# A hybrid decoder layer on one core: S5 tables made earlier and stored in longer runs, the last stage's weights split once

## The chip, the core and the metric

The kernel runs on one core of one Trainium2 chip. The metric is the time of one execution on the device in microseconds. TensorE (PE) multiplies matrices, VectorE (DVE), ScalarE (ACT) and GpSimd (POOL) work on elements, and SyncE (SP) issues the DMAs. All names in capitals are those of the profile.

## The reference

One layer with 2048 tokens of 1024 channels in float32. The input is normalized and projected to 8716 columns; three branches use them: A, a diagonal complex state space model (S5) with 32 groups of 16 channels and 64 states each; B, dilated window attention; C, a Mamba-2 SSD scan. Each branch is gated, projected, weighed by a sigmoid gate and summed; one more projection is added to the input. Cut to what matters:

```python
h = rms_norm(x, norm_w)
proj = h @ w_in
(u_a, z_a, q, k, v, z_b, xbc, dt, z_c, gate_logits) = split(proj, ...)
y_a = s5_mixer(u_a, ...) * silu(z_a)
y_b = attention_mixer(q, k, v, ...) * silu(z_b)
y_c = ssd_mixer(xbc, dt, z_c, ...)
gates = sigmoid(gate_logits)              # three of 1024 columns
merged = g0 * (y_a @ proj_a) + g1 * (y_b @ proj_b) + g2 * (y_c @ proj_c)
return x + merged @ w_out

def s5_mixer(u, ...):
    lam, f = ...                          # per group and state, complex
    bu = einsum(f * b, u)
    h[t] = lam * h[t - 1] + bu[t]         # a scan over 2048 tokens
    y = real(einsum(c, h)) + d * u
    g = gelu(y)
    return g * sigmoid(g @ glu_w + glu_b)
```

## The kernel before

**Precision.** Every large matmul is made in three passes of fp32r: each operand is split in a high part (rounded, made on ACT) and a low part (the rest, made on DVE), and TensorE adds high x high, low x high and high x low (L373 to L375, L384 to L386, L1267 to L1269).

**The projection** runs in two halves of 1024 tokens, in units of one output tile each; a unit is 24 matmuls, with 256 or 512 columns. For each weight tile one DMA of 1 MB brings the raw columns (`wr_q`, `wr_k`, `wr_g`, ..., L345), ACT casts them to the high part (L360), DVE makes the low part (L361). Outputs go to DRAM (`q_d`, `k_d`, `v_d`, `ua_d`, `g_d`, ...).

**Branch work between the units.** `main` calls `run` with jobs (work, its steps, first unit, last unit), and the steps of a job are spread evenly over these units. In this way the S5 parameters come first (`s5_setup`, units 2 to 38), then attention and the SSD chunks of the first half (`ssd(0)`, units 73 to 135), h of the second half (`a0_early`, from unit 84), then in the second half the S5 branch itself (`s5`, units 153 to 180), its GLU, attention, and SSD chunks (`ssd(1)`). The final order of each engine's instructions is set by the compiler's scheduler from this program; all DMAs stand in one queue on SP, in program order as it was scheduled, and use eight semaphores in turn.

**S5.** `s5_setup` writes a table `tab_d` of [128, 32 groups, 163 columns] to DRAM with ten DMAs, each in a slice of 16 to 19 columns, that is, in runs of 64 to 76 bytes (L935, L940, L952, L967, L1015). `s5` works in eight blocks of four groups. For each it loads the table (`s5t`), and `cplx` (L1042 to L1044) makes three sets of complex products, with two POOL multiplies and one DVE add each; TensorE turns one of them (`s5pp`) and makes the lag kernels from another (`s5kp`, L1062), which go through DRAM (`ks_d`). The phasors `wt` take eight POOL multiplies (L1102, L1103) and four DVE operations (L1104) a block. Then, group by group: a matmul (`s5i`, L1112), the turn back on DVE and POOL, a scan on DVE (L1121), the turn forward, and two matmuls (`s5yp`, L1132 and L1133).

**SSD.** For each chunk, POOL makes the rows `sr` (L806) that TensorE needs for `sd` (L811); their results go on to `syd`, `syo`, `ssp` on TensorE.

**The last stage** (`final`) does four time blocks of 512 tokens. Each has eight projection steps: a step loads 128 columns of `proj_a`, `proj_b`, `proj_c` as three DMAs (`fr`, 768 KB), splits them on ACT (L1197, L1257) and DVE (L1198, L1258), does 36 matmuls of 512 columns (`fp`, L1267 to L1269), and weighs the three results by the gates `fg`, loaded from `g_d` (L1264), on DVE (L1270) and POOL (L1272). Then come four output steps: 1 MB of `w_out` (`or`), four splits, 96 matmuls of 256 columns (`op`, L1302 to L1304). The same weights are loaded and split anew in each of the four time blocks. SSD chunks and the attention merge of the second half run beside its first blocks (`last`).

## Time and profile before

| | |
|---|---|
| time, median of 3 runs | 2605.06 us (2604.53 to 2605.40) |
| span of the profiled execution | 2611.2 us, 40810 instructions |
| busy: PE, DVE, ACT, POOL | 2477.1, 1465.2, 888.8, 718.3 us |
| DMA | 354.90 MB in 463591 packets, mean 136 GB/s |

The profile is of one execution of its own; its span is its time, and there is no other figure for it. PE's busy time is the whole time in which it had a matmul under way. PEclk is the TensorE clock that was granted, as a part of full speed. DMA share is the mean busy share of the 16 DMA engines. "Idle before" names what ended the idle time of the engine ahead of an instruction.

### The profile page before, as it was taken

Reading aid. Unit: us, or ns where it says so; the run is one execution under the profiler, and the core shown is the slowest. Engines: PE = TensorE matmul, PEld = TensorE weight load, DVE = VectorE, ACT = ScalarE, POOL = GpSimd, SP = SyncE. Lnnn points to the kernel's source line nnn. Section 1 sums busy time; section 2 is a strip of 40 time slices with the busy share of each in tenths; the row PEclk is TensorE's granted clock in tenths of the full one; section 3 lists DMA queues with packets and bytes.
Section 4 is the critical chain, followed back from the end, with each engine's and each line's share of the span. In section 5 each row is a group of like instructions: output and inputs, shape, how many; then the busy total and the mean of one; then the engine's idle time right before and its main releaser. Section 6 shows DMA issues by size and latency. Waiting matters only on the chain. (4 is left out here: it accounts for less than half of the span.)

```text
span 2611.2 us, 40810 instructions
## 1 busy us (share of the span) xinstructions
PE 2477.1 (95%) x15216; PEld 2173.1 (83%) x15216; DVE 1465.2 (56%) x3153; ACT 888.8 (34%) x1956; POOL 718.3 (28%) x737
## 2 busy tenths in 40 slices
PE   8778999999999999978889999999999999999999
PEld 8778998888888888877789998888888779797888
DVE  6652255643433335488986546642333887878663
ACT  4122234543233224212225335443332433333331
POOL 2121000002333324288862100000010343534221
PEclk8988999999999999999999999999999999999999
DMA  7995332433445335343336432443343667675664
GB/s 156 90 56 117 100 108 83 138 117 108 134 145 158 119 103 166 81 111 106 101 97 198 127 119 90 138 138 105 117 137 123 212 201 218 200 214 169 204 201 133
DMA packets 463591, 354.90 MB, mean 136 GB/s; under 512 B 132641, under 2 KB 420641, under 8 KB 463393
## 3 DMA queue, kind: packets, MB, share of 16 engines
q1 hardware_dynamic: 463392, 352.29, 50.6%
q8 instruction: 121, 1.98, 0.3%
q14 instruction: 78, 0.63, 0.1%
HBM read 239.79 MB, written 112.41 MB: 135 GB/s over the span
## 5 line engine op out<-in xcount | busy, mean ns | idle before, releaser
L384 PE MATMUL ps_g<-hT_hi,wh_g 128*128 128x512 f32 x768 | 310.0, 404 | 0.0
L386 PE MATMUL ps_g<-hT_hi,wl_g 128*128 128x512 f32 x768 | 305.6, 398 | 0.0
L385 PE MATMUL ps_g<-hT_lo,wh_g 128*128 128x512 f32 x768 | 305.0, 397 | 0.0
L806 POOL TENSOR_TENSOR sr<-tle,ahl 128x384 fp32r<-128x384 f32 x128 | 116.3, 930 | 519.9 <-PE sd L811 388.5
L386 PEld LDWEIGHTS ps_g<-hT_hi,wl_g 128*128 128x128 f32 x768 | 144.5, 188 | 33.1
L385 PEld LDWEIGHTS ps_g<-hT_lo,wh_g 128*128 128x128 f32 x768 | 144.5, 188 | 32.3
L384 PEld LDWEIGHTS ps_g<-hT_hi,wh_g 128*128 128x128 f32 x768 | 144.4, 188 | 32.2
L1272 POOL TENSOR_TENSOR fm<-fm,fg 128x512 f32<-128x512 f32 x64 | 96.0, 1500 | 209.7 <-DVE fg L1270 172.6
L361 DVE TENSOR_TENSOR wl_g<-wr_g,wh_g 128x512 fp32r<-128x512 f32 x96 | 71.0, 759 | 116.1 <-ACT wh_g L360 106.3
L659 ACT ACTIVATE sm<-sm,ml 128x256 f32<-128x256 f32 (+1 forms) x192 | 86.4, 451 | 136.1 <-DVE ml L657 111.9
L373 PE MATMUL ps_q<-wh_q,hT_hi 128*128 128x256 f32 x384 | 112.5, 294 | 18.0 <-ACT e_q L424 17.6
L384 PE MATMUL ps_xbc<-hT_hi,wh_xbc 128*128 128x512 f32 x320 | 129.0, 403 | 0.0
L385 PE MATMUL ps_xbc<-hT_lo,wh_xbc 128*128 128x512 f32 x320 | 128.6, 402 | 0.0
L386 PE MATMUL ps_xbc<-hT_hi,wl_xbc 128*128 128x512 f32 x320 | 128.4, 401 | 0.0
L373 PE MATMUL ps_v<-wh_v,hT_hi 128*128 128x256 f32 x384 | 110.7, 291 | 13.2 <-ACT e_v L414 10.8
L374 PE MATMUL ps_v<-wl_v,hT_hi 128*128 128x256 f32 x384 | 112.9, 295 | 9.5 <-DVE wl_v L361 9.5
L563 ACT ACTIVATE e_g<-ps_g 128x512 f32<-128x512 f32 x96 | 56.9, 595 | 182.3 <-PE ps_g L386 173.8
L498 DVE SCALAR_TENSOR_TENSOR ac_cv<-xb_cv,convw,ac_cv 128x512 f32<-128x512 f32 x120 | 90.3, 752 | 48.9 <-ACT ac_cv L496 48.2
L374 PE MATMUL ps_k<-wl_k,hT_hi 128*128 128x256 f32 x384 | 112.0, 292 | 5.8 <-DVE wl_k L361 5.7
L374 PE MATMUL ps_q<-wl_q,hT_hi 128*128 128x256 f32 x384 | 112.5, 294 | 4.6 <-DVE wl_q L361 4.6
L373 PE MATMUL ps_k<-wh_k,hT_hi 128*128 128x256 f32 x384 | 112.1, 294 | 4.8 <-ACT e_k L424 4.8
L375 PE MATMUL ps_q<-wh_q,hT_lo 128*128 128x256 f32 x384 | 113.4, 296 | 3.3 <-DVE hT_lo L317 3.3
(627 smaller groups left out, 7552.5 us busy)
## 6 DMA issues: line engine op xcount, KB each, us to landing
wr_g<-in_w_in_dram SPq DMA_DIRECT2D x24, 1024.0 KB, 5.3
g_d<-e_g SPq DMA_DIRECT2D x96, 256.0 KB, 2.4
fg<-g_d SPq DMA_DIRECT2D x96, 256.0 KB, 5.3
or<-in_w_out_dram SPq DMA_DIRECT2D x16, 1024.0 KB, 5.8
fr<-in_proj_c_dram SPq DMA_DIRECT2D x32, 384.0 KB, 5.1
wr_xbc<-in_w_in_dram SPq DMA_DIRECT2D x10, 1024.0 KB, 5.4
x<-in_x_dram SPq DMA_DIRECT2D x32, 256.0 KB, 3.9
wr_uz<-in_w_in_dram SPq DMA_DIRECT2D x8, 1024.0 KB, 5.4
```

What stands on the lines that cost most here:

```text
L361: nc.vector.tensor_sub(l[:, :, :n], s, h[:, :, :n].bitcast(F32))
L373: nc.tensor.matmul(ps, hi[:, t], wh, start=kt == 0, stop=False)
L374: nc.tensor.matmul(ps, hi[:, t], wl, start=False, stop=False)
L375: nc.tensor.matmul(ps, lo[:, t], wh, start=False, stop=kt == KT - 1)
L384: nc.tensor.matmul(ps, wh, hi, start=kt == 0, stop=False)
L385: nc.tensor.matmul(ps, wh, lo, start=False, stop=False)
L386: nc.tensor.matmul(ps, wl, hi, start=False, stop=kt == KT - 1)
L498: nc.vector.scalar_tensor_tensor(acc, xb[:, k:k + 512], cw[:, ct, k:k + 1], acc, op0=ALU.mult, op1=ALU.add)
L563: nc.scalar.activation(e, ps, AF.Tanh, scale=0.5)
L659: nc.scalar.activation(sm[:, h], sm[:, h], AF.Exp, bias=ml[:, h:h + 1], accum_out=ob[:, h, 64:65])
L806: nc.gpsimd.tensor_mul(r, self.tle.unsqueeze(1).to_broadcast([P, 3, P]), ahl[:, i, h0:h0 + 3].unsqueeze(2).to_broadcast([P, 3, P]))
L1272: nc.gpsimd.tensor_add(acc, acc, gt)
```

## The change

**Tables in longer runs.** `tab_d` becomes [128, 8 blocks, 4 x 162 columns]: the four groups of a block lie together for each table, so that a write is in runs of 256 or 288 bytes. The modulus goes to a tensor of its own, `rho_d`.

```diff
-        self.tab_d = dram("tab_d", [P, 32, TABW])
+        self.tab_d = dram("tab_d", [P, 8, 4 * TABW])
+        self.rho_d = dram("rho_d", [P, 32])
+        self.p1_d = dram("p1_d", [P, 32, P])
+        self.o1_d = dram("o1_d", [P, 32, P])
+        self.wt_d = dram("wt_d", [P, 32, 2, 256])
+        self.pw_d = dram("pw_d", [8, P, 2, 12, P])
+        self.wo_d = dram("wo_d", [4, P, 2, 8, 256])
...
+        def put(off, wd, src):
+            nc.sync.dma_start(self.tab_d[:, :, off * 4:(off + wd) * 4], src)
...
-        nc.sync.dma_start(tab[:, :, 128:147], w)
+        put(128, 18, w.rearrange("p (b g) k -> p b (g k)", b=8))
```

**Tables in the first half.** A new generator `s5_tables` (40 steps) does, block by block, what the first part of a block did in `s5`: the multiplies on POOL, the adds on DVE, the transposes and `s5kp` on TensorE, and writes `p1_d` (256 KB), `ks_d`, `o1_d` (256 KB) and `wt_d` (two writes of 512 KB). `s5` (42 steps in place of 66) only loads them, and keeps the work group by group.

```diff
+            x1 = cplx("x", rev[:, :, 0:8], rev[:, :, 8:16], b1, b2)
...
+            nc.sync.dma_start(self.p1_d[:, gs, :], p1)
...
+                for q, (x, y, f) in enumerate(((0, 16, v.tensor_sub), (16, 0, v.tensor_add))):
+                    gp.tensor_mul(v16(wt[:, :, q, :]), hi16(32), lo16(x))
+                    gp.tensor_mul(v16(tmp), hi16(48), lo16(y))
+                    f(wt[:, :, q, :], wt[:, :, q, :], tmp)
+                nc.sync.dma_start(self.wt_d[:, b * 4 + pr * 2:b * 4 + pr * 2 + 2], wt)
+                yield
...
+            p1 = t4("p1", self.p1_d[:, gs, :])
+            wt = t4("w", self.wt_d[:, gs], (P, 4, 2, 256))
+            t0 = t4("t0", None)
```

**Weights split once.** `out_weights` (20 steps) loads the rows of `proj_a`, `proj_b`, `proj_c` and `w_out` in tiles of 128 x 1024 (512 KB), splits each with one ACT and one DVE instruction, and writes the high and the low part: `pw_d` with 24 writes, `wo_d` with 16, each 512 KB. In `final` a step loads both parts with one DMA: 1.5 MB for a projection step, 2 MB for an output step, in one run of 12 or 16 KB a partition; `split` is gone. The pool `wp` of the projection's weights is closed ahead of the last stage, and the pool of these loads takes its place.

```diff
+    def fw(self, name, src, kn, n):
+        t = self.fp.tile([P, 4096], F32R, name=name, tag="fw", bufs=2)
+        t = t[:, :2 * kn * n].rearrange("p (x k n) -> p x k n", x=2, n=n)
+        self.nc.sync.dma_start(t.bitcast(F32), src)
+        return [(t[:, 0, k, :], t[:, 1, k, :]) for k in range(kn)]
...
-                for w, k0, k1 in ((pa, 0, 4), (pb, 4, 6), (pc, 6, 12)):
-                    nc.sync.dma_start(raw[:, k0:k1, :], w[:, :, cs])
...
+                W = self.fw(f"fp{nm}", self.pw_d[dt], 12, P)
...
+                W = self.fw(f"fo{nm}", self.wo_d[cg], 8, 256)
```

**The spread of the jobs.**

```diff
-        run([(self.ssd(0), 66, 73, 135), (chain(self.attention(0, 0), self.attention(1, 0)), 40, 41, 80),
-             (self.a0_early(), 8, 84, 120)], 136)
+        ssd0, early0 = self.ssd(0), self.a0_early()
+        run([(early(ssd0, 10), 10, 73, 82), (chain(self.attention(0, 0), self.attention(1, 0)), 40, 41, 80)], 82)
...
+        run([(early(ssd0, 36), 36, 83, 116), (self.s5_tables(), 40, 83, 115), (early0, 8, 84, 115)], 116)
...
+        run([(ssd0, 20, 117, 135), (self.out_weights(), 20, 117, 134)], 136)
...
-        run([(self.s5(), 66, 153, 180)], 180)
+        run([(self.s5(), 42, 153, 180)], 180)
```

**Three places of the order.** First SP's queue in the setup, between the key units and the load of the next key weights (`v_d` is the store of the values, `wr_k` the load). Before:

```order
L935 DMA tab_d_92<-s5w_1268 4096x1x19
L417 DMA v_d0_69<-e_v0_0_0_1192 128x2x256
L417 DMA v_d0_69<-e_v0_0_1_1244 128x2x256
L952 DMA tab_d_92<-s5bb0_1395 4096x1x16
L952 DMA tab_d_92<-s5bb1_1401 4096x1x16
L417 DMA v_d0_69<-e_v0_1_0_1340 128x2x256
L417 DMA v_d0_69<-e_v0_1_1_1392 128x2x256
L345 DMA wr_k1_0_1774<-in_w_in_dram 128x8x256
```

And now:

```order
L882 DMA tab_d_92<-s5w_1275 1024x1x72
L425 DMA v_d0_69<-e_v0_0_0_1198 128x2x256
L425 DMA v_d0_69<-e_v0_0_1_1250 128x2x256
L882 DMA tab_d_92<-s5bb0_1401 1024x1x64
L882 DMA tab_d_92<-s5bb1_1407 1024x1x64
L425 DMA v_d0_69<-e_v0_1_0_1346 128x2x256
L425 DMA v_d0_69<-e_v0_1_1_1398 128x2x256
L353 DMA wr_k1_0_1780<-in_w_in_dram 128x8x256
```

The writes stand at the same places; their shape changes from 4096 runs of 16 or 19 words to 1024 of 64 or 72.

Second, POOL where SSD chunk 1 of the first half is made (`sr1_3`, `sr1_6`: its rows for TensorE's `sd1_3` and `sd1_6`; `s5x`, `s5k`, `s5o` and their `t` twins, `s5w`, `s5wt`: the table multiplies). Before:

```order
L806 TENSOR_TENSOR sr1_3_0_6774<-tle_396,ahl0_6104 128x384
L806 TENSOR_TENSOR sr1_3_1_6776<-tle_396,ahl0_6104 128x384
L787 TENSOR_TENSOR sxd1_6646<-sx1_6636,dt0_5982 128x768
L788 TENSOR_TENSOR sx1_6636<-sx1_6636,hpar_417 128x768
L790 TENSOR_TENSOR sxdd1_6649<-sxd1_6646,edc0_6113 128x768
L237 TENSOR_SCALAR sss0_6590<-sss0_6590 128x1
L238 TENSOR_TENSOR sss0_6590<-sss0_6590,nhalf_98 128x1
L806 TENSOR_TENSOR sr1_6_0_6861<-tle_396,ahl0_6104 128x384
L806 TENSOR_TENSOR sr1_6_1_6863<-tle_396,ahl0_6104 128x384
```

And now, a little further down, ahead of the same pair `sr1_6`:

```order
L1060 TENSOR_TENSOR s5x1_6942<-s5t1_6940 128x512
L1105 TENSOR_TENSOR s5wt0_1_6892<-s5t0_6668 128x512
L1104 TENSOR_TENSOR s5w1_0_7112<-s5t1_6940 128x2x256 x2
L1061 TENSOR_TENSOR s5ot1_7044<-s5t1_6940 128x512
L1105 TENSOR_TENSOR s5wt0_1_6892<-s5t0_6668 128x512
L1060 TENSOR_TENSOR s5k1_6955<-s5t1_6940 128x512
L1105 TENSOR_TENSOR s5wt1_0_7113<-s5t1_6940 128x512
L1060 TENSOR_TENSOR s5o1_7043<-s5t1_6940 128x512
L814 TENSOR_TENSOR sr1_6_0_6930<-tle_402,ahl0_6110 128x384
L814 TENSOR_TENSOR sr1_6_1_6932<-tle_402,ahl0_6110 128x384
```

Of the instructions between `sr1_3` and `sr1_6`, 23 are now table multiplies of blocks 0 and 1. TensorE's `s5pp0` stands ahead of `sd1_3` in its order, and `sd4_9` of chunk 4 right behind the last block's work.

Third, SP's queue in the first time block of the last stage (`fr`, `fp`: weights of a step; `fg`: gates). Before:

```order
L1264 DMA fg0_3_0_20256<-g_d_83 128x512 [waits DMAHW3_49,Pool_49]
L1244 DMA fr0_5_20465<-in_proj_a_dram 128x4x128 [waits DMAHW4_49,DVE_49]
L1244 DMA fr0_5_20465<-in_proj_b_dram 128x2x128 [waits DMAHW5_49]
L1244 DMA fr0_5_20465<-in_proj_c_dram 128x6x128 [waits DMAHW6_49]
L1264 DMA fg0_3_1_20272<-g_d_83 128x512 [waits DMAHW7_49]
L1264 DMA fg0_3_2_20283<-g_d_83 128x512 [waits DMAHW0_49,Pool_49]
L1264 DMA fg0_4_0_20377<-g_d_83 128x512 [waits DMAHW1_49]
L1244 DMA fr0_6_20568<-in_proj_a_dram 128x4x128 [waits DMAHW2_49,DVE_49]
```

And now:

```order
L1282 DMA fp0_5_20575<-pw_d_97 128x3072 [waits DMAHW1_49,PE_49]
L1297 DMA fg0_4_1_20503<-g_d_83 128x512 [waits DMAHW2_49]
L1297 DMA fg0_4_2_20514<-g_d_83 128x512 [waits DMAHW3_49,Pool_49]
L1297 DMA fg0_5_0_20578<-g_d_83 128x512 [waits DMAHW4_49,Pool_49]
L1282 DMA fp0_6_20652<-pw_d_97 128x3072 [waits DMAHW5_49,PE_49]
L790 DMA sct13_21859<-cmT_d_82 128x2x128 [waits DMAHW6_49,PE_49]
L1297 DMA fg0_5_1_20594<-g_d_83 128x512 [waits DMAHW7_49,Pool_49]
```

A step's weights were three loads that waited for DVE, which had split the ones before; they are now one load that waits for TensorE, and gates of the step before and of its own stand behind it.

## Rows read from the trace of the kernel before

**Rows 1.** The page, part 1: busy us (share of the span) x instructions.

```profile
PE 2477.1 (95%) x15216; PEld 2173.1 (83%) x15216; DVE 1465.2 (56%) x3153; ACT 888.8 (34%) x1956; POOL 718.3 (28%) x737
```

**Rows 2.** Busy time by stretch: us, PE, PEld, DVE, ACT, POOL, PEclk, DMA share, GB/s.

```profile
100.00:250.00 150.00, 108.67 (x817) 107.64 (x816) 56.00 (x220) 26.54 (x47) 26.08 (x24) 0.84 0.97 89
250.00:300.00 50.00, 50.00 (x425) 50.00 (x424) 12.16 (x19) 12.59 (x23) 7.33 (x8) 1.00 0.29 91
```

**Rows 3.** Waits of ScalarE, 0 to 250 us: us in total, times, longest.

```profile
ACT wh_k L360 <- DMA wr_k<-in_w_in_dram: 40.9, 3, 32.4
```

**Rows 4.** Timeline of SP's queue, 50 to 130 us: start, duration, instruction.

```profile
99.40 9.85 SPq L952 DMA_DIRECT2D tab_d<-s5bb  x2
109.34 11.95 SPq L417 DMA_DIRECT2D v_d<-e_v  x2
121.38 0.42 SPq L345 DMA_DIRECT2D wr_k<-in_w_in_dram  x1
```

**Rows 5.** DMA issues by name: count, KB each, median us to landing.

```profile
wr_g<-in_w_in_dram SPq DMA_DIRECT2D x24, 1024.0 KB, 5.3
...
x<-in_x_dram SPq DMA_DIRECT2D x32, 256.0 KB, 3.9
...
ua_d<-e_uz SPq DMA_DIRECT2D x16, 256.0 KB, 2.6
...
tab_d<-s5ph SPq DMA_DIRECT2D x4, 256.0 KB, 17.6
...
tab_d<-s5bb SPq DMA_DIRECT2D x2, 256.0 KB, 23.2
```

**Rows 6.** Waits of TensorE, 100 to 250 us: us in total, times, longest.

```profile
PE ps_q L373 <- ACT e_q L424: 17.6, 1, 17.6
...
PE ps_v L374 <- DVE wl_v L361: 5.0, 1, 5.0
...
PE ps_k L374 <- DVE wl_k L361: 3.1, 1, 3.1
```

**Rows 7.** Busy time by stretch (columns of rows 2): the S5 stage.

```profile
1100.00:1400.00 300.00, 254.82 (x1828) 238.57 (x1827) 257.65 (x381) 78.79 (x146) 233.13 (x227) 0.94 0.41 111
```

**Rows 8.** Costliest groups, 1100 to 1400 us: busy, mean ns | idle before.

```profile
L1103 POOL TENSOR_TENSOR s5wt<-s5t 128x512 f32<-128x512 f32 x27 | 34.6, 1281 | 2.8 <-DVE s5w L1104 2.5
...
L1104 DVE TENSOR_TENSOR s5w<-s5w,s5wt 128x512 f32<-128x512 f32 x28 | 30.5, 1088 | 4.2 <-POOL s5w L1102 4.0
```

**Rows 9.** Busy time by stretch: the first half's gates units.

```profile
700.00:1000.00 300.00, 300.00 (x1412) 245.75 (x1411) 109.08 (x152) 92.71 (x182) 91.12 (x105) 1.00 0.43 134
```

**Rows 10.** Costliest groups of POOL, 650 to 1080 us.

```profile
L806 POOL TENSOR_TENSOR sr<-tle,ahl 128x384 fp32r<-128x384 f32 x50 | 40.8, 837 | 132.3 <-PE sd L811 132.3
...
L788 POOL TENSOR_TENSOR sx<-sx,hpar 128x768 f32<-128x768 f32 x6 | 10.6, 1774 | 0.2
...
L1102 POOL TENSOR_TENSOR s5w<-s5t 128x512 f32<-128x512 f32 x4 | 5.6, 1418 | 0.0
L238 POOL TENSOR_TENSOR xs<-xs,nhalf 128x1 f32<-128x1 f32 x7 | 4.4, 626 | 0.6
...
L1042 POOL TENSOR_TENSOR s5x<-s5t 128x512 f32<-128x512 f32 x2 | 2.2, 1088 | 4.7 <-DMA s5t<-tab_d 4.7
```

**Rows 11.** Timeline of TensorE, 715 to 735 us: start, duration, instruction.

```profile
715.83 0.39 PE L384 MATMUL ps_g<-hT_hi,wh_g 128*128 128x512 f32 x1
...
717.69 0.39 PE L386 MATMUL ps_g<-hT_hi,wl_g 128*128 128x512 f32 x1
...
731.90 0.81 PE L851 MATMUL spt<-ident,sx 128*128 128x128 f32 x6
732.48 0.48 PE L385 MATMUL ps_g<-hT_lo,wh_g 128*128 128x512 f32 x1
```

**Rows 12.** Busy time by stretch: the last stage's first three time blocks.

```profile
2050.00:2490.00 440.00, 410.08 (x2347) 354.40 (x2348) 345.83 (x626) 169.24 (x385) 172.60 (x141) 0.97 0.67 205
```

**Rows 13.** Waits of TensorE, 2050 to 2550 us.

```profile
PE fp L1267 <- DVE fg L1270: 11.1, 7, 2.9
```

More of the change, by code (lines that the diff above doesn't have):

```diff
@@ L939, in s5_setup @@
             nc.vector.tensor_copy(w[:, :, 1, 7 - n], li[:, :, n])
[L940 removed]
+        put(146, 16, w.rearrange("p (b g) a n -> p b (g a n)", b=8))
         yield
@@ L951, in s5_setup @@
             (sub if i else add)(o, o, t)
-            nc.sync.dma_start(tab[:, :, 64 + 16 * i:80 + 16 * i], o)
+            put(64 + 16 * i, 16, o.rearrange("p (b g) k -> p b (g k)", b=8))
         yield
@@ L1188, in s5_glu, with out_weights @@
             nc.sync.dma_start(rows(self.ya_d), q)
-    def split(self, name, src, scale, kn, n, hi_tag="wh", lo_tag="wl"):
-        nc = self.nc
-        h = self.wp.tile([P, 2, 268], F32R, name=f"{name}h", tag=hi_tag, bufs=6)
-        l = self.wp.tile([P, 2, 268], F32R, name=f"{name}l", tag=lo_tag, bufs=6)
-        h, l = (a.rearrange("p a b -> p (a b)")[:, :kn * n].rearrange("p (k n) -> p k n", n=n) for a in (h, l))
-        nc.scalar.activation(h, src, AF.Copy, scale=scale)
-        nc.vector.scalar_tensor_tensor(l, src, scale, h.bitcast(F32), op0=ALU.mult, op1=ALU.subtract)
-        return h, l
+    def out_weights(self):
+        nc, A = self.nc, self.A
+        for j in range(20):
+            if j < 4:
+                src, k, scale = A["proj_a"], j, 0.125
+            elif j < 6:
+                src, k, scale = A["proj_b"], j - 4, 0.5
+            elif j < 12:
+                src, k, scale = A["proj_c"], j - 6, self.snw[:, j - 6:j - 5]
+            else:
+                src, k, scale = A["w_out"], j - 12, 0.5
+            raw = self.ct(f"ow{j}", [P, D], tag="ow", bufs=2)
+            nc.sync.dma_start(raw, src[0, k * P:(k + 1) * P, :])
+            hl = self.ct(f"owh{j}", [P, 2, D], F32R, tag="owh", bufs=2)
+            nc.scalar.activation(hl[:, 0], raw, AF.Copy, scale=scale)
+            nc.vector.scalar_tensor_tensor(hl[:, 1], raw, scale, hl[:, 0].bitcast(F32),
+                                           op0=ALU.mult, op1=ALU.subtract)
+            for x in range(2):
+                if j < 12:
+                    dst = self.pw_d[:, :, x, j, :].rearrange("t p c -> p t c")
+                    nc.sync.dma_start(dst, hl[:, x].bitcast(F32).rearrange("p (t c) -> p t c", c=P))
+                else:
+                    dst = self.wo_d[:, :, x, j - 12, :].rearrange("t p c -> p t c")
+                    nc.sync.dma_start(dst, hl[:, x].bitcast(F32).rearrange("p (t c) -> p t c", c=256))
+            yield
     def load_y(self, tb):
@@ L1285, in final @@
                 nm = f"{tb}_{cg}"
-                raw = self.wp.tile([P, KT, 268], F32, name=f"or{nm}", tag="wr", bufs=1)
-                nc.sync.dma_start(raw[:, :, 0:256], wo[:, :, cg * 256:(cg + 1) * 256])
-                W = []
-                for j in range(4):
-                    h, l = self.split(f"o{nm}_{j}", raw[:, 2 * j:2 * j + 2, 0:256], 0.5, 2, 256)
-                    W += [(h[:, k, :], l[:, k, :]) for k in range(2)]
+                W = self.fw(f"fo{nm}", self.wo_d[cg], 8, 256)
                 def rows(d, pr):
```

199 lines of the change are left out of this document (95 added, 104 removed).

## The prediction

> **What bounds the kernel now.** I read the page first: TensorE is busy 95% of the span [rows 1], so time can come only from the stretches where it is not. Next, busy time by stretch. It is short of work in three places. In the setup, 100 to 250 us, it is busy 108.67 of 150 us at a granted clock of 0.84, and from 250 us on it is full at 1.00 [rows 2]. Its 817 matmuls there would take 96 us at the 425 per 50 us of the full row, so 54 us are lost: 41 to idling, 13 to the lower clock. In the S5 stage, 1100 to 1400 us, it idles 45 of 300 us, with VectorE at 257.65 and GpSimd at 233.13 [rows 7]. In the last stage, 2050 to 2490 us, it idles 30 us, with the DMA engines at 0.67 [rows 12]. From 700 to 1000 us it never stops, with GpSimd at 91 of 300 [rows 9].
>
> Then the waits, for who is late. In the setup ScalarE waits 40.9 us for `wr_k` in three pieces, 32.4 the longest [rows 3]; TensorE's 17.6 behind `e_q` [rows 6] is the same delay, since `e_q` stands behind the cast on ScalarE. The SP timeline shows why the weights are late: two table writes hold SP for 9.85 us at 99.40, the v_d writes behind them for another 11.95, and `wr_k` is issued only at 121.38 [rows 4]. A table write of 256 KB in runs of 64 bytes lands after 17.6 to 23.2 us; 256 KB in runs of 256 bytes (`ua_d`) after 2.6 [rows 5].
>
> **The parts of the change.** The sum is made on the profiled execution, whose span is 2611.2 us, 6.1 above the median 2605.06 of the runs; I subtract the gain from the median.
>
> *Setup writes.* Ten writes go from 4096x1x16 to 1024x1x64, the very shape of `ua_d`, so 2.6 us each instead of some 20 [rows 5]; the extra `rho_d` write (16 KB, 128 runs) is below a table write in every respect, and I put it at nothing while the queue is free. The weights stop being late. What is late next is the VectorE split: 5.0 us for `wl_v` and 3.1 for `wl_k` are waited for already now [rows 6]. Of 54 us I keep back these 8 and 4 more for the first weights: **+42**. Ends: +54 if nothing is late; +25 if the splits' waits triple.
>
> The Trainium skill, "DMA: Bandwidth & Descriptors", Specifications, says that transfers below 512 bytes miss line rate because the DMA engine reads and rewrites; by that alone runs of 256 bytes would still be slow, and this term would be near 0, and the sum too. The trace has 16 writes of just this shape at 2.6 us [rows 5], and the measurement decides. It is the third rival below.
>
> *S5 stage.* Gone from it are 112 GpSimd multiplies (64 of L1102/L1103 and 48 of L1042/L1043) at 1.28 us [rows 8], 143 us with those that ran before 1100; gone from VectorE are 32 adds of 1.09 [rows 8] and 24 like them, 61 us. Of the busy times of 1100 to 1400 that leaves about 200 us for VectorE and 115 for GpSimd (an estimate: most of these operations lie in these 300 us), in the 255 us that TensorE needs: no longer the bound. What is late next is the chain of one block, which crosses VectorE and GpSimd four times. Gain **+42** of 45; ends +30 and +58 (all idling, and 13 us more from a clock of 0.94 that returns to 1). The new loads, 1.5 MB a block in place of the 326 KB table, go beside DMA at 0.41 [rows 7]: nothing; without that cover, 5 us a block.
>
> *Tables in the first half.* The 143 us of GpSimd work move into units 83 to 115. In the order, from `s5x0` to the pair `sr4_9`, GpSimd does 110 multiplies x 1.28 [rows 8] = 141, 28 `sr` x 0.84 = 23.5, 12 state and `sx` operations of the same width, 10, 12 `sxd`, `sx` and `sxdd` of double width at about 1.77, 21, and 20 of one column, 0.4 on average with 0.63 the largest, 9 [rows 10]: 205 us. TensorE, from `s5pp0` to `sd4_9`, does 612 matmuls of 512 columns at 0.2325 (eight steps from start to start in 1.86 us [rows 11]) = 142, and about 30 us of small ones (six transposes cost 0.58 [rows 11]): 172. Table multiplies stand ahead of the `sr` pairs that TensorE's `sd` waits for, so the difference becomes idling: **-33**. Ends: the multiplies at 1.09, as the first ones run, give 184, so -12; at 1.42, as the last ones before 1080 run [rows 10], 220, so -50 with 2 for the bunching. The 56 adds on VectorE (61 us) and the drains on ScalarE go beside engines busy 109 and 93 of 300 [rows 9]: nothing. The writes, some 13 MB in 215 us, take 60 GB/s beside 134 at a DMA share of 0.43 [rows 9]: nothing, but they queue on SP ahead of `wr_g`.
>
> *Weights split once.* Twenty loads of 512 KB and 40 writes of 512 KB in units 117 to 134, 31.5 MB in about 18 x 6.9 = 124 us (the 6.9 is a unit of 24 matmuls, 5.6 us, plus its share of branch work). With the 134 GB/s that flow there now, 48 MB. At 0.43 for 134 GB/s [rows 9] full DMA is 312 GB/s, so 154 us in 124. The overflow of 30 builds up over the stretch, and a `wr_g`, which serves four units, stands two to three units ahead of its use in the order, some 18 us: **-10**; ends 0 (4 KB loads move faster) and -31. ScalarE and VectorE take 20 splits of 1024 columns, about 2 us each, beside the shares above: nothing.
>
> *Start of the last stage.* The tiles of the split weights lie where the projection's weights lay, so the first 1.5 MB load waits for the last gates matmul. A load of 256 KB lands in 3.9 us and one of 1 MB in 5.3 [rows 5]; on that line 1.5 MB takes 6.2; a few branch matmuls fill some of it: **-8**, ends -3 and -15.
>
> *Last stage.* Out go the splits, eight operations a projection step and four an output step on VectorE and as many on ScalarE. The largest wait of TensorE is 11.1 us for `fg` on VectorE [rows 13]; with smaller ones behind VectorE and ScalarE I take 23 of the 30 us for theirs (estimate). In come 10.5 MB more for each time block. A projection step is 36 matmuls x 0.2325 = 8.4 us. Its load is issued when the step two before has ended (the order shows the wait on PE), and must land within one step: 6.2 us, behind 0.75 MB of `fg` at 312 GB/s (2.5) and merge and SSD traffic (0.8): 9.5, so 1.1 us too late in 24 steps of the first three blocks, 27 us if none of it overlaps. I take half, 14: **+9**; ends +27 and -30.
>
> Sum: 42 + 42 - 33 - 10 - 8 + 9 = **+42**: a span near 2569, a median near **2563 us**.
>
> **Rivals.**
> 1. *Most costs hide.* GpSimd's table multiplies run at the short end and the loads land in time: 54 + 45 - 12 - 3 - 3 + 23 = +104, 2501. For it: GpSimd is at 30% there [rows 9] and the DMA at 0.67 in the last stage [rows 12]. Against: the order bunches the tables. It needs all ends at once; a part of it, 2520 to 2540, is likelier. Chance 0.22 for below 2540.
> 2. *Slower: the single DMA queue becomes the bound of the last stage.* The first three blocks move 205 GB/s x 440 us = 90 MB at a share of 0.67 [rows 12], which makes 306 GB/s when full; with 31.5 MB more, 122 MB need 398 us, when TensorE is busy 410. There is no slack, and each load starts only after a step's end. If loads and `fg` don't overlap at all, a projection step is 1.5 MB at 306 (5.1) + 2 to start (1 MB: 5.3 less 3.4) + 3.3 = 10.4, 2.0 late in 32 steps (64 us), and an output step 2.1 MB, 6.9 + 2 + 4 = 12.9 against 96 matmuls of half the columns, 11.2, 1.7 late in 16 (27 us). With +23 of relief that is -68 here, and with -31 and -33 before it the sum is 42 + 42 - 33 - 31 - 8 - 68 = -56: 2661. It decides once the last stage loses over 33 us net in place of my +9. For it: the wait on PE in the order. Against: runs of 12 KB should move faster than the mixture does. Chance 0.11.
>
>    The Trainium skill, "DMA: Bandwidth & Descriptors", Bandwidth, gives 6.15 us for 1 MB and 79.0 for 16 MB, from which 1.5 MB would be an estimated 8.6 us: more than a step by itself. The trace's 1 MB in 5.3 us [rows 5] is already shorter.
> 3. *The setup is not relieved* (the writes stay slow, or VectorE holds the weights): +42 becomes 0 and the sum 0, 2605. Against: [rows 5]. Chance 0.05.
> 4. *GpSimd at its dear end and the weights' queue too*: 42 + 42 - 50 - 31 - 8 + 9 = +4, up to 2601. Chance 0.12 for 2585 to 2600.
>
> **How the numbers follow.** The forecast, 2540 to 2585, has 0.50. What a measurement can tell from no change is 0.2%, 5 us. Faster: the forecast, rival 1 and rival 4, 0.50 + 0.22 + 0.12 = 0.84, less 0.01 for the edge: 0.83. Same: 0.05 from rival 3. Slower: 0.12. The range runs from 2505 to 2612: it leaves out the end of rival 1 (about 0.07) and most of rival 2 (0.11).
>
> **What would show it.** Right: `tab_d` writes near 2.6 us and the granted clock near 1 from 100 to 250 us; in the S5 stage TensorE idle under 10 us with GpSimd near 40%; in the first half 20 to 50 us of new idling, put down to GpSimd's `sr` before `sd`; in the last stage no wait for split weights on VectorE, and some for `fp` loads. Wrong: TensorE full through the table stage (rival 1); `fp` or `fo` loads that take over 8.4 us and lead the list of waits (rival 2); ScalarE still waiting for `wr_k` (rival 3).

## The result and the profile after

The changed kernel takes 2518.36 us (median of 4, 2515.12 to 2529.26) against 2604.80 (2603.34 to 2605.40): ratio 0.967, 95% interval 0.965 to 0.969, 86 us less. The forecast was 2563 us. The side was right, and the size was not: the gain of 86 us is twice the forecast 42.

The span of the profiled execution is 2516.5 us, 2 below the median; that of the kernel before was 6 above its own. So the two traces differ by 94.7 us and the times by 86: some 8 us of what the traces show come from an execution of the kernel before that was slower than its median.

Both traces have the same 11712 matmuls of the projection and the last stage, in the same order. The table gives the start of some of them in the timelines of TensorE, in us; the lead of the change is the difference. The other matmuls, those of the branches, need not stand at the same places in both, which matters in the last stage (see there).

| matmul | before | after | lead | in this stretch | forecast |
|---|---|---|---|---|---|
| 1440, end of the setup | 254.2 | 198.4 | 55.8 | +55.8 | +42 |
| 3120, before the table stage | 596.5 | 540.9 | 55.6 | 0 | 0 |
| 4080, behind it | 868.2 | 858.2 | 10.0 | -45.6 | -33 |
| 4800, behind the weights' split | 1054.0 | 1043.9 | 10.1 | 0 | -10 |
| 6720, behind the S5 stage | 1442.1 | 1367.2 | 74.9 | +64.8 | +42 |
| 8880, in the last gates units | 2019.4 | 1944.7 | 74.7 | 0 | 0 |
| 9600, in the first output steps | 2193.6 | 2133.2 | 60.4 | -14.3 | -8 |
| 11711, the last one | 2607.0 | 2512.5 | 94.5 | +34.1 | +9 |

The page of the changed kernel: busy time of TensorE; in 40 slices its clock and the GB/s moved.

```profile
PE 2453.7 (98%) x15216; PEld 2158.3 (86%) x15216; DVE 1336.7 (53%) x2852; ACT 783.9 (31%) x1656; POOL 708.7 (28%) x737
...
PEclk8999999999999999999999999999999999999999
...
GB/s 169 128 107 98 104 103 101 154 87 181 176 181 178 335 355 233 139 144 173 174 165 152 127 106 92 148 124 128 112 126 112 227 303 308 290 286 264 306 290 223
```

TensorE is busy 98% in place of 95% [rows 1]. Busy time by stretch (columns of rows 2):

```profile
100.00:250.00 150.00, 150.00 (x1271) 150.00 (x1270) 65.81 (x215) 40.41 (x69) 33.41 (x32) 1.00 0.35 109
540.00:850.00 310.00, 292.11 (x1368) 234.44 (x1367) 196.10 (x234) 95.22 (x192) 234.88 (x209) 0.96 0.59 187
1050.00:1350.00 300.00, 290.56 (x2183) 280.13 (x2182) 205.63 (x341) 92.95 (x168) 120.55 (x147) 0.99 0.54 156
1100.00:1250.00 150.00, 144.16 (x1069) 138.44 (x1068) 109.36 (x209) 38.62 (x76) 67.13 (x95) 0.99 0.62 175
1990.00:2400.00 410.00, 391.52 (x2327) 345.94 (x2328) 228.59 (x374) 69.85 (x135) 161.22 (x141) 0.98 0.85 293
```

The setup is full, at a clock of 1.00 with a DMA share of 0.35, where 108.67 of 150 us, 0.84 and 0.97 stood [rows 2]. The table stage, 540 to 850, is new: GpSimd 235 and VectorE 196 of 310 us, TensorE idle for 18. In the S5 stage GpSimd falls to 120.55 of 300 us and TensorE idles 9, where it idled 45 [rows 7]. In the last stage the DMA share is 0.85, after 0.67 [rows 12], and VectorE falls to 229 of 410.

DMA issues, KB each and median us to landing, for [rows 5]:

```profile
fp<-pw_d SPq DMA_DIRECT2D x32, 1536.0 KB, 6.8
fo<-wo_d SPq DMA_DIRECT2D x16, 2048.0 KB, 8.7
...
fg<-g_d SPq DMA_DIRECT2D x96, 256.0 KB, 7.0
pw_d<-owh SPq DMA_DIRECT2D x24, 512.0 KB, 6.5
...
tab_d<-s5ph SPq DMA_DIRECT2D x4, 256.0 KB, 3.3
...
tab_d<-s5bb SPq DMA_DIRECT2D x2, 256.0 KB, 3.6
```

The table writes land in 3.3 and 3.6 us instead of 17.6 and 23.2. SP's timeline, for [rows 4]:

```profile
88.22 1.25 SPq L882 DMA_DIRECT2D tab_d<-s5bb  x2
91.52 6.00 SPq L425 DMA_DIRECT2D v_d<-e_v  x2
97.61 0.42 SPq L353 DMA_DIRECT2D wr_k<-in_w_in_dram  x1
```

The two writes hold SP for 1.25 us, not 9.85, and `wr_k` is issued at 97.61 instead of 121.38.

TensorE's waits (total, times, longest), first from 600 to 1000, then 1000 to 1400, then 1900 to 2516 us:

```profile
PE xT L295 <- DVE x L289: 14.9, 7, 4.6
```

```profile
PE s5yp L1167 <- POOL s5r L1164: 5.4, 5, 1.8
```

```profile
PE op L1333 <- DVE fm_lo L1313: 7.2, 2, 4.2
PE syd L828 <- DVE sm L822: 5.6, 1, 5.6
PE op L1331 <- DMA fo<-wo_d: 2.8, 2, 2.6
...
PE fp L1300 <- DVE fg L1303: 0.5, 1, 0.5
```

No table is waited for any more in the S5 stage. In the last stage the wait for `fg` is 0.5 us [rows 13: 11.1], and the new loads cost 2.8 us in two pieces, both for `fo`: no wait is put down to the 1.5 MB loads (`fp`, 6.8 us to land, where 6.2 were worked out). What the first of them costs is e13's question.

### The profile page after: what moved, and what is told of

The parts are those of the page before. It is cut to its first block, busy times and chain, and to the rows that moved or that the text cites. A ratio compares the mean times of both kernels' runs of the same rounds, so it can differ in the third digit from the quotient of the medians.

```text
span 2516.5 us, 40172 instructions
## 1 busy us (share of the span) xinstructions
PE 2453.7 (98%) x15216; PEld 2158.3 (86%) x15216; DVE 1336.7 (53%) x2852; ACT 783.9 (31%) x1656; POOL 708.7 (28%) x737
## 4 chain that ended last, share of the span: by engine, by line
PE 55%; DMA 6%; DVE 5%; POOL 4%; SPq 2%; issue 1%; ACT 1%; DVEq 0%; ACTq 0%; POOLq 0%
PE ps_g L392 5%; PE ps_g L394 5%; PE ps_g L393 5%; PE fp L1300 3%; PE fp L1302 3%; PE fp L1301 3%; PE op L1333 2%; PE op L1331 2%; PE op L1332 2%; PE ao L688 2%; PE ps_xbc L393 2%; PE ps_xbc L394 1%; PE ps_xbc L392 1%; PE as L659 1%; PE ps_uz L394 1%
## 5 line engine op out<-in xcount | busy, mean ns | idle before, releaser
L814 POOL TENSOR_TENSOR sr<-tle,ahl 128x384 fp32r<-128x384 f32 x128 | 122.1, 977 | 440.0 <-PE sd L819 305.9
L394 PEld LDWEIGHTS ps_g<-hT_hi,wl_g 128*128 128x128 f32 x768 | 144.9, 189 | 33.5 <-issue 0.5
L1300 PE MATMUL fp<-fy_hi,fp 128*128 128x512 f32 x384 | 154.3, 402 | 0.5 <-DVE fg L1303 0.5
L1333 PE MATMUL op<-fo,fm_lo 128*128 128x256 f32 x512 | 146.3, 287 | 7.2 <-DVE fm_lo L1313 7.2
L1331 PE MATMUL op<-fo,fm_hi 128*128 128x256 f32 x512 | 147.8, 289 | 4.9 <-DMA fo<-wo_d 2.8
L1302 PE MATMUL fp<-fy_hi,fp 128*128 128x512 f32 x384 | 151.3, 394 | 0.0
L1301 PE MATMUL fp<-fy_lo,fp 128*128 128x512 f32 x384 | 150.9, 393 | 0.0
L1332 PE MATMUL op<-fo,fm_hi 128*128 128x256 f32 x512 | 146.5, 286 | 0.0
L1305 POOL TENSOR_TENSOR fm<-fm,fg 128x512 f32<-128x512 f32 x64 | 85.5, 1336 | 206.6 <-DVE fg L1303 190.9
L369 DVE TENSOR_TENSOR wl_g<-wr_g,wh_g 128x512 fp32r<-128x512 f32 x96 | 77.2, 826 | 92.2 <-ACT wh_g L368 91.9
```

The costliest lines, as they stand in the source:

```text
L394: nc.tensor.matmul(ps, wl, hi, start=False, stop=kt == KT - 1)
L814: nc.gpsimd.tensor_mul(r, self.tle.unsqueeze(1).to_broadcast([P, 3, P]), ahl[:, i, h0:h0 + 3].unsqueeze(2).to_broadcast([P, 3, P]))
L1300: nc.tensor.matmul(ps, W[k][0], yh[k], start=k == k0, stop=False)
L1301: nc.tensor.matmul(ps, W[k][0], yl[k], start=False, stop=False)
L1302: nc.tensor.matmul(ps, W[k][1], yh[k], start=False, stop=k == k1 - 1)
L1331: nc.tensor.matmul(ps, mh[k][:, t], W[k][0], start=k == 0, stop=False)
```

## The experiments

All ratios are to the kernel before on the same chip; its median there was 2594 to 2599 us. "Lead" is against the kernel before's trace, at the matmuls of the table.

**The layout alone (e1).** The kernel before; `tab_d` [P, 8, 4 x 162] with the writes of the change, `rho_d`, and the S5 stage reading slices of it.

```diff
-            w = self.ct(f"s5t{b}", [P, 4, TABW], tag="s5tab", bufs=2)
-            nc.sync.dma_start(w, self.tab_d[:, gs, :])
+            w = self.ct(f"s5t{b}", [P, 4 * TABW], tag="s5tab", bufs=2)
+            nc.sync.dma_start(w, self.tab_d[:, b, :])
```

> The kernel before with the new layout of tab_d alone (writes in runs of 256 bytes, the modulus in a tensor of its own; the tables are still made in the S5 stage). Theory 1 (the late weight loads were the whole loss of the setup): all of the 55.7 us that the changed kernel is ahead at the end of the setup come from this edit: about 2549 us, ratio 0.979. Rival (VectorE, relieved of other work or put in another order, gives part of it): under 40 us, above 2565. If the S5 stage moves too, its table loads were late, which nothing shows: then below 2540.

2551.75 us, ratio 0.9825 (0.981 to 0.9839). The lead is 55.8 us at the end of the setup and stays there; 6 more come in the S5 stage. The stretch of the setup is that of the full change:

```profile
100.00:250.00 150.00, 150.00 (x1270) 150.00 (x1269) 65.51 (x214) 40.53 (x69) 33.44 (x32) 1.00 0.35 109
```

In time the whole kernel gains 45 us, not 56, and about 39 without the S5 stage: the size that the rival gave, though not for its reason. The kernel with the weights alone (e3) has the setup of before, word for word, and lost 14 us less there than the profiled execution of before:

```profile
100.00:250.00 150.00, 120.56 (x924) 119.53 (x923) 58.17 (x212) 30.74 (x53) 31.57 (x30) 0.87 0.82 91
```

So the loss in the setup differs between executions, 120.56 us busy here and 108.67 in [rows 2], and the profile of before showed a dear one; these are two executions, and whether the chip or the moment makes the difference isn't shown. The rival falls: nothing but the writes was changed there, and the lead is the same.

**The tables without the weights (e2).** The change with the last stage of before and no split ahead:

```diff
-        run([(ssd0, 20, 117, 135), (self.out_weights(), 20, 117, 134)], 136)
+        run([(ssd0, 20, 117, 135)], 136)
```

> The changed kernel without the weights split ahead: the last stage loads and splits as before, units 117 to 134 carry only SSD chunks. Theory 1 (the parts add up): 55.7 of the setup, and 64.7 - 45.6 of the S5 stage and the table stage, so about 75 us less than before, 2530 us, ratio 0.971. Rival (the split ahead costs DMA time between 850 and 950 us that the last stage hides): lower than that, near 2520 or below, and the full change then gains little from its second part.

2535.23 us, ratio 0.9769 (0.9741 to 0.9797). Leads: 55.4, then -47.8 in the table stage and +61.1 in the S5 stage. Theory 1's 0.971 lies outside the interval, by about as much as the traces of the setup show more than the times; the rival's lower time didn't come. Moving the tables is worth 0.56% beside e1, some 15 us net.

**The weights without the tables (e3).** The kernel before, SSD chunks at 73 to 116 and 117 to 135 and h of the second half at 84 to 115, with `out_weights` at 117 to 134 and the last stage of the change.

> The kernel before with the weights split ahead alone (units 117 to 134) and the last stage of the changed kernel. Theory 1: the traces show 74.6 us at the last stage's start and 94.5 at its end, so this part is worth 20 us: 2585 us, ratio 0.992, with no wait of TensorE for wr_g between 850 and 1000 us. Rival (loads of 1.5 MB become the bound, as the prediction's second rival had it, and only the other parts' relief pays): 2605 or more.

2579.08 us, ratio 0.9926 (0.991 to 0.9943): 17 to 19 us, about as expected. The trace shows no wait of TensorE at all from 700 to 1000 us, so the split ahead is free. The new spread of the jobs is not quite: between matmuls 3120 and 4080 e3, without any tables, loses 5 us, 3.5 of them in a wait for `xT`. The lead falls by 10 us at the start of the last stage and rises by 33.5 from there. The gains of e2 and e3 add up to 3.05%; the full change has 3.0 to 3.3%.

**The second half's h behind the tables (e4).**

```diff
-        run([(early(ssd0, 36), 36, 83, 116), (self.s5_tables(), 40, 83, 115), (early0, 8, 84, 115)], 116)
+        run([(early(ssd0, 36), 36, 83, 116), (self.s5_tables(), 40, 83, 115)], 116)
...
-        run([(ssd0, 20, 117, 135), (self.out_weights(), 20, 117, 134)], 136)
+        run([(ssd0, 20, 117, 135), (self.out_weights(), 20, 117, 134), (early0, 8, 117, 134)], 136)
```

> The changed kernel with h of the second half (a0_early) made in units 117 to 134 in place of 84 to 115. In the changed kernel TensorE waits 14.9 us between 600 and 1000 us for its transposes' input, which VectorE scales after a power on GpSimd. Theory 1 (GpSimd is full between 560 and 800 us, and everything that has to pass it is late): these waits go, others for the SSD rows take part of their place: 5 to 15 us less than the changed kernel, 2505 to 2513. Rival A (only these tiles' own chain is slow): all 15 us go, 2503. Rival B (the waits come back as waits for SSD in full, since the queue on GpSimd is as long without them): 2516 to 2520.

2527.31 us, ratio 0.9726 (0.971 to 0.9743): slower than the change. The waits changed their name (TensorE, 540 to 1100 us):

```profile
PE spt L859 <- DVE sx L853: 16.7, 4, 6.5
PE xT L295 <- DVE x L289: 5.7, 3, 3.0
```

`spt` belongs to the SSD chunks; its waits lie before 850 us, those of `xT` now behind. The waits came back under another name, as rival B had it, and more was lost behind: against the change this kernel is 9 us ahead at matmul 4080 and 9 behind at 4560. The 9 us are no relief: the 64 transposes `xT` that have left the stage took 9.7 us there, and TensorE idles 21 us in it, not fewer than the 18 of the change. Beside the weights' split, at a DMA share of 1.07 from 850 to 950 us, the eight steps cost 19 us, about 7 of them the transposes and about 7 idling.

**A part of the multiplies on VectorE (e5).**

```diff
-                    gp.tensor_mul(v16(tmp), hi16(48), lo16(y))
+                    v.tensor_mul(v16(tmp), hi16(48), lo16(y))
```

> The changed kernel with 32 of the 112 table multiplies (the second product of each phasor) on VectorE in place of GpSimd. Theory 1 (GpSimd's work bounds the table stage): 32 x 1.28 = 41 us leave GpSimd, which was 272 us busy in 403, and VectorE, 243 busy, takes 32 x about 1 us; most of the 18 us of idling and of the lower clock go: 15 to 30 us less than the changed kernel, ratio near 0.958. Rival (VectorE is the late one there, as the name of the wait says, or the time is TensorE's own moved work): no gain or a loss, ratio 0.967 to 0.972.

2516.87 us, ratio 0.9698 (0.9678 to 0.9718), beside 0.9700 (0.9677 to 0.9723) for the change itself on that chip:

> The changed kernel again, beside the three runs above on one chip. Theory 1: ratio 0.967, as first measured, with 94 us in the traces' difference and about 86 in the times. No rival of the mechanism; it fixes what the others are compared with.

No gain: theory 1 falls, and with it the prediction's reason, that GpSimd's work alone sets the price. From 540 to 850 us:

```profile
540.00:850.00 310.00, 290.48 (x1378) 235.24 (x1377) 221.37 (x266) 95.73 (x194) 207.64 (x177) 0.96 0.59 188
```

28 us have left GpSimd and 25 have come to VectorE; TensorE idles 19.5 us in place of 18. The moved multiplies take 1.34 us on VectorE, a little more than on GpSimd (1.22 in the change):

```profile
L1105 DVE TENSOR_TENSOR s5wt<-s5t 128x512 f32<-128x512 f32 x32 | 42.9, 1341 | 6.1 <-DMA s5t<-tab_d 5.6
...
L289 DVE TENSOR_SCALAR x<-x,xs 128x512 f32<-128x512 f32 x16 | 11.9, 783 | 5.0 <-POOL xs L246 5.0
```

**The tables over more units (e6).**

```diff
-        run([(early(ssd0, 10), 10, 73, 82), (chain(self.attention(0, 0), self.attention(1, 0)), 40, 41, 80)], 82)
+        run([(chain(self.attention(0, 0), self.attention(1, 0)), 40, 41, 71)], 72)
...
-        run([(early(ssd0, 36), 36, 83, 116), (self.s5_tables(), 40, 83, 115), (early0, 8, 84, 115)], 116)
+        run([(early(ssd0, 46), 46, 73, 116), (self.s5_tables(), 40, 73, 115), (early0, 8, 84, 115)], 116)
```

> The changed kernel with the tables over units 73 to 115 in place of 83 to 115, and attention of the first half over units 41 to 71 in place of 41 to 80, so that the two don't share the memory. Theory 1 (in 33 units GpSimd has more work than TensorE, in 43 it has less): the table multiplies thin out from 3.4 to 2.6 a unit, GpSimd needs about 250 us in 43 x 6.8 = 292, and TensorE's idling between 540 and 830 us falls from 18 to under 8 us, with a clock near 1: 15 to 30 us less than the changed kernel, ratio 0.956 to 0.961. Rival (attention, packed denser, gets late on VectorE and ScalarE and takes it back): ratio 0.965 or more, with new waits before 550 us.

2510.55 us, ratio 0.9675 (0.9655 to 0.9695). The four times, 2509 to 2513, lie below the four of the change on that chip, 2514 to 2518, but the intervals overlap: a gain of 6 us is likely and not certain. It is not what either side forecast. TensorE idles 17 of 310 us, not under 8, so theory 1 falls here too. The rival's late attention isn't there either; from 250 to 560 us TensorE waits once:

```profile
PE syd L828 <- DVE sm L822: 1.8, 1, 1.8
```

And the multiplies were not thinned out: they start at 521 us instead of 558 and end at 771 instead of 799, so they take 250 us instead of 241. The scheduler put them forward in a block. What a thinner table stage costs, e6 doesn't tell.

**Less work in the table stage (e9).**

```diff
-                    gp.tensor_mul(v16(tmp), hi16(48), lo16(y))
-                    f(wt[:, :, q, :], wt[:, :, q, :], tmp)
```

> The changed kernel with the second product of each phasor and its add left out: 32 GpSimd multiplies and 32 VectorE adds fewer in the table stage; the phasors are not the reference's, everything else is done. Moving 32 multiplies to VectorE saved nothing, and the traces show both engines' operations getting longer beside each other (the scaling of x on VectorE 484 ns before, 1025 now, 783 with the multiplies moved). Theory 2 (the sum of the two engines' work bounds the stage, since they slow each other): with 41 + 45 us less of it the idling of 18 us falls below 6 and the clock returns: 20 to 30 us less than the changed kernel, ratio 0.959 to 0.962. Rival (the order: table work stands ahead of the chains of xT and spt, however long it takes; or TensorE's own moved work of 12 us is the loss): at least 12 us of idling stay, under 12 us gained, ratio 0.965 or more.

2487.16 us, ratio 0.9569 (0.9551 to 0.9588), a little below theory 2's range: 30 us less in the table stage (lead at matmul 4080: 40.5 us).

```profile
540.00:850.00 310.00, 307.95 (x1504) 250.18 (x1504) 160.63 (x220) 104.95 (x206) 197.66 (x190) 1.00 0.69 220
```

TensorE idles 2 us, its clock is 1.00. The rival falls: the order alone, or TensorE's own moved work, would have kept 12 us. Theory 2 fits both runs: moving 32 operations between the two engines changes nothing, leaving them out with their adds brings back 30 of the 45.6 us. But e9 takes work off both engines at once, and it takes out something else too. In the change (540 to 850 us) VectorE stands idle ahead of just these adds, waiting for the second products:

```profile
L1106 DVE TENSOR_TENSOR s5w<-s5w,s5wt 128x512 f32<-128x512 f32 x32 | 45.2, 1414 | 20.1 <-POOL s5wt L1105 20.1
```

What stands behind such an add in VectorE's order, the scaling for `xT` included, may be held with it. No run leaves out the products alone or the adds alone, so the sum of the work, this chain between the engines, and each engine being late in its turn are not told apart.

**The second half's h beside attention (e11).** `early0` at units 48 to 81.

> The changed kernel with h of the second half (a0_early, 8 steps) made in units 48 to 81, beside attention, in place of 84 to 115. It takes eight token tiles' scaling, transposes (64, about 8 us of TensorE) and drains out of the table stage, and puts them where TensorE had no idle time and GpSimd is idle. Theory 2: VectorE is free enough beside attention (some 30 of 50 us), so the moved work costs only TensorE's 8 us there, as it did before, and the table stage loses its waits at xT without new ones: 8 to 20 us less than the changed kernel, ratio 0.960 to 0.966. Rival (as when it was moved behind the tables: the waits come back at spt, behind the same queues): ratio 0.968 or more.

2512.18 us, ratio 0.9671 (0.9654 to 0.9688), between the two ranges: no clear gain. In the trace the rival holds: the waits came back at `spt` (TensorE, 300 to 1000 us), and from 540 to 850 us TensorE idles 22 us, though 64 of its matmuls are gone from there:

```profile
PE spt L859 <- DVE sx L853: 16.9, 5, 6.7
```

**The tables over more units, the split elsewhere (e12).** Tables at 83 to 134 (52 units in place of 33), the weights' split at 137 to 176, SSD chunks and h spread as before the change.

```diff
-        run([(self.s5(), 42, 153, 180)], 180)
+        run([(self.out_weights(), 20, 137, 176), (self.s5(), 42, 153, 180)], 180)
```

> The changed kernel with the tables spread over units 83 to 134 (SSD chunks and h of the second half as in the kernel before), and the weights' split moved to units 137 to 176, in the second half, where the pool of the S5 stage has room. Theory 2 (the sum of VectorE's and GpSimd's work per unit bounds the table stage): the table work falls from 3.4 to 2.2 multiplies a unit, TensorE's idling there from 18 to under 5 us and its clock stays near 1; of the 44 us that the stage costs now, the 12 of TensorE's own moved work stay and 25 to 32 go; the 20 splits and 63 MB of the weights cost the S5 stage at most 8: 17 to 30 us less than the changed kernel, ratio 0.957 to 0.963. Rival (the scheduler bunches the tables at the front of any window, as in the run with units 73 to 115): under 8 us less, ratio above 0.965.

2527.94 us, ratio 0.9724 (0.9707 to 0.9742): slower than the change, where 17 to 30 us less were expected. Here the multiplies were spread, from 558 to 878 us. The lead on the change is 9 us behind the table stage (matmul 4800), not 25 to 32, and from 540 to 900 us TensorE still idles 14 us, not under 5:

```profile
540.00:900.00 360.00, 345.77 (x1644) 279.45 (x1643) 198.04 (x253) 105.78 (x214) 250.34 (x232) 0.98 0.51 163
```

So theory 2 fits e5 and e9 and got e12 wrong in size: with the busy time of the two engines down from 1.39 to 1.25 us in each us (431 in 310, 448 in 360; in e9 1.16), some of the idling went, not most of it. And between matmuls 4800 and 6720, the S5 stage, e12 lost 21 us on the change:

```profile
1100.00:1250.00 150.00, 128.61 (x900) 121.51 (x900) 103.16 (x190) 39.96 (x75) 63.03 (x84) 0.94 0.83 250
```

TensorE is busy 128.61 of 150 us, 144.16 in the change, with the DMA share at 0.83 instead of 0.62. The same 20 steps that cost nothing beside the gates cost 21 us beside S5, whose pieces of 64 KB from `ua_d` come through the same queue and land after 4.6 us in place of 2.6. TensorE's largest wait there is for `s5yp` behind GpSimd's `s5r`, 13.3 us; whether the queue or the splits on VectorE and ScalarE made it late wasn't tried.

**The splits' operations kept (e7).**

```diff
+            self.nc.scalar.activation(dh[:, :w], src, AF.Copy, scale=0.5)
+            self.nc.vector.scalar_tensor_tensor(dl[:, :w], src, 0.5, dh[:, :w].bitcast(F32),
+                                                op0=ALU.mult, op1=ALU.subtract)
```

> The changed kernel with the operations of the splits kept in the last stage: eight ScalarE and eight VectorE instructions a projection step, four and four an output step, on the loaded tiles; their results are not used. Theory 1 (the last stage was bound by VectorE's work around the gates, and the loads are not in the way): of the 34 us that the last stage gained after its start, 20 to 30 are lost again, ratio 0.975 to 0.979. Rival (the gain came from loads in long runs that land in time): under 8 us lost, ratio below 0.970.

2540.57 us, ratio 0.979 (0.9771 to 0.981): 24 us more than the change on that chip (e8), 23 of them in the trace behind matmul 8880, as theory 1 had it in sum. But 13 of the 23 lie before matmul 9600 and only 10 behind it, where theory 1 looked for them. The stretch and the waits are much like those of before again, with the loads of the change:

```profile
1990.00:2400.00 410.00, 375.91 (x2142) 325.60 (x2141) 340.51 (x607) 156.08 (x372) 165.73 (x141) 0.97 0.82 280
```

```profile
PE op L1343 <- DVE fm_lo L1323: 9.8, 3, 5.2
PE fp L1310 <- DVE fg L1313: 8.5, 9, 1.7
```

So the work of the splits on VectorE and ScalarE was the loss, and the loads of 1.5 and 2 MB are not in the way even at 0.82.

**The first load of the last stage (e13), and its control (e14).** A buffer of its own for the first load; to make room, 7 evacuation buffers instead of 9, which e14 has alone.

```diff
-        t = self.fp.tile([P, 4096], F32R, name=name, tag="fw", bufs=2)
+        if name == "fp0_0":
+            t = self.f0.tile([P, 3072], F32R, name=name, tag="fw0", bufs=1)
+        else:
+            t = self.fp.tile([P, 4096], F32R, name=name, tag="fw", bufs=2)
```

> The changed kernel with the last stage's first load (1.5 MB) in a buffer of its own, so that it need not wait for the projection's last matmul; to make room the evacuation buffers are 7 in place of 9. The alignment of the traces shows that the changed kernel falls back by 14 us against the kernel before between the last gates unit and the first output step. Theory 3 (the prediction's term of 8 us for the start: TensorE fills the landing of that load with branch matmuls that are not ready): 6 to 14 us of it come back against the run with 7 buffers alone, about 2505. Rival (the SSD chunk and the attention merge, which share these steps, are late in any case; the wait of 5.6 us for sm on VectorE says so): under 4 us.

> The changed kernel with 7 evacuation buffers in place of 9, and nothing else: what the run above is compared with. Theory 3 and its rival alike: within 3 us of the changed kernel, ratio 0.967 to 0.971; if it is more, the buffers held the gates' drains, and the run above is read against this one.

2514.88 us, ratio 0.9679 (0.9651 to 0.9707), against 2518.02, 0.9689 (0.9656 to 0.9722). In the traces e13 wins 9 us against e14 between matmuls 8880 and 9600, 5 of them less idling and the rest mostly branch matmuls that run later, and 5 us are left at the end. In the times it is 3, under the rival's 4, and the intervals cover each other: that the load's wait costs some 5 us is what the traces say, the times can't tell.

## Where the prediction was right, and where it was wrong

The prediction was wrong in size: the traces show some 53 us more gain than its sum of +42. By the table, 14 of them lie in the setup, 10 in the two stages of the tables together, 10 in the weights' split and 19 in the last stage with its start.

**Setup: right in cause, +42 against 55.8 in the trace and about 40 in time.** Twelve us were kept back for VectorE and the first weights; from 100 to 250 us TensorE then waited for nothing. The times of e1 give 45 with the 6 of the S5 stage, because the execution that was profiled lost more than others did. So the 12 kept back were wrong for that trace, and the term near right for the times, which is luck.

**Tables moved: +9 forecast for both stages together, +19 came.** Two things were left out of the sum, which nearly cancel between the stages. One is TensorE's own part of the tables. In the changed kernel's timeline a block's `s5pp` and `s5kp` put off the next projection matmul by 1.51 us:

```profile
584.40 0.60 PE L1068 MATMUL s5pp<-ident,s5x 128*128 128x128 f32 x4
584.93 1.05 PE L1077 MATMUL s5kp<-s5k,s5t 128*16 128x128 f32 x8
585.91 0.50 PE L392 MATMUL ps_uz<-hT_hi,wh_uz 128*128 128x512 f32 x1
```

Eight blocks make about 12 us that leave the S5 stage and come to the table stage. The other is the clock: granted 0.94 in the S5 stage before [rows 7] and 0.96 in the table stage now, in each case where TensorE idles, and 1.00 in e9, where it doesn't. Of the 45.6 us of the table stage 18 are idling, 12 moved work, and the rest, some 15, goes with the clock; the S5 stage gives back 37, 12 and about 15. The shares of the clock are what is left over, not measured by themselves. The -33 forecast for idling alone was nearly twice too much, and the 10 us by which the pair came out better are idling: 18 in place of 33, less 37 in place of 42.

**Its reason was wrong too.** The step that failed is "Table multiplies stand ahead of the `sr` pairs that TensorE's `sd` waits for, so the difference becomes idling", GpSimd's 205 us against TensorE's 172. e5 takes 32 of the multiplies, 41 us by that sum, off GpSimd; 164 would be less than 172 and no idling left, but 19.5 us are. And TensorE waits for `xT` behind the scaling of x on VectorE, 14.9 us in the change, not for `sd`. The longest of these waits, 4.6 us, ends at 603.9 us, and GpSimd's order has its part in it: the scale `xs` of that tile has its last step there behind two table multiplies, and then two scalings on VectorE follow:

```profile
599.86 2.06 POOL L1104 TENSOR_TENSOR s5w<-s5t 128x512 f32<-128x512 f32 x2
601.88 0.56 POOL L246 TENSOR_TENSOR xs<-xs,nhalf 128x1 f32<-128x1 f32 x1
```

```profile
602.48 2.46 DVE L289 TENSOR_SCALAR x<-x,xs 128x512 f32<-128x512 f32 x2 [1.88 <-POOL xs L246]
```

So what the runs put in the place of GpSimd's work alone is the work of both engines, which this chain crosses (e5, e9); how much its order adds to its amount is not settled (e9, e12). VectorE's groups (busy, mean ns), of the kernel before from 650 to 950 and of the change from 540 to 850 us:

```profile
L361 DVE TENSOR_TENSOR wl_g<-wr_g,wh_g 128x512 fp32r<-128x512 f32 x44 | 35.4, 821 | 45.4 <-ACT wh_g L360 40.5 <-PE sd L811 4.9
...
L281 DVE TENSOR_SCALAR x<-x,xs 128x512 f32<-128x512 f32 x14 | 8.6, 656 | 5.4 <-POOL xs L238 5.4
```

```profile
L369 DVE TENSOR_TENSOR wl_g<-wr_g,wh_g 128x512 fp32r<-128x512 f32 x32 | 31.1, 992 | 18.0 <-ACT wh_g L368 17.9
...
L289 DVE TENSOR_SCALAR x<-x,xs 128x512 f32<-128x512 f32 x16 | 15.8, 1026 | 4.5 <-POOL xs L246 3.5 <-DMA p_d<-s5p 0.9
```

The same operations are longer where GpSimd is busy 76% of the time than where it is busy a third: 656 and 1026 ns for the scaling of x, 821 and 992 for the low parts; 783 in e5, where GpSimd has less to do. The Trainium skill, "GPSIMD Engine Reference", Specifications, says that GpSimd shares its SBUF interfaces with VectorE and that the two contend when VectorE's instruction has two SBUF inputs or runs in a 2-port mode. The low parts, which have two such inputs, agree; in which mode the scaling runs, no run here shows.

The means hide two lengths. In VectorE's timelines a scaling of x takes either 0.47 to 0.49 us or over 1 us, mostly 1.27 to 1.29; every one without a GpSimd operation beside it is short, and every long one stands beside one. Two of 16 are long in the kernel before, 11 in the change, 6 in e5. But 11 are long in e9 too, where TensorE doesn't idle. So the lengthening is shown, and that it is what TensorE waits for is not. e4 and e11 add that taking the late work out of the stage only renames the wait.

**Weights split ahead: 0 instead of -10.** The estimate of 312 GB/s at a full share was too low for these transfers: the slices of the page from 818 to 944 us reach 335 and 355 GB/s, and no `wr_g` was late. e12 shows that the split isn't free at every place.

**Last stage with its start: +20 instead of +1, the largest miss.** The table's -14.3 and +34.1 must not be read as the price of the start and the worth of the relief. From matmul 8880 to 9600 and from there to the end, before and after (columns of rows 2):

```profile
2019.40:2193.60 174.20, 162.08 (x861) 136.75 (x860) 143.57 (x276) 65.75 (x148) 73.29 (x62) 0.97 0.65 200
2193.60:2607.00 413.40, 393.22 (x2331) 344.15 (x2330) 291.33 (x533) 147.41 (x344) 134.23 (x107) 0.98 0.63 193
```

```profile
1944.70:2133.20 188.50, 173.52 (x950) 147.26 (x950) 139.76 (x262) 45.35 (x93) 94.11 (x85) 0.97 0.82 272
2133.20:2512.50 379.30, 371.47 (x2242) 330.85 (x2241) 149.46 (x227) 44.47 (x78) 100.83 (x85) 0.99 0.81 280
```

In the change 89 more matmuls, all of SSD chunks and the merge, run ahead of matmul 9600 and as many fewer behind it: some 16 us that only changed their place. TensorE idles 15.0 us in place of 12.1 in the first stretch and 7.8 in place of 20.2 in the second. What can be compared is the sum, +20; 9.5 of it are less idling, the rest was not taken apart.

The relief was forecast at 23, and e7, which puts the splits' operations back, loses 23: that term was right in size (e7's operations load the engines, but nothing waits for their results). The step that failed is the 14 us for loads that land too late, and with it the 8 for the start: of the 22, 3 are left. The load (6.8 us) and the gates (7.0) overlap in the queue, they don't add up, and all waits for loads come to 2.8 us. The first load costs some 5 us in the traces of e13 and e14; what offsets it is not shown.

**The rivals.** The first (most costs hide, 2501 to 2540) names the time that came, and describes the setup, the split and the last stage; its table stage, -12, came as -45.6, and part of that was made up by the clock and the matmuls that left the S5 stage, which it didn't count. The second falls: the DMA share went to 0.85, and the loads are waited for 2.8 us. The third fell with the first row of the SP timeline. The fourth had the table stage (-50) and got the weights' queue (-31) wrong.
